# Eight gate blocks of a hybrid encoder step, computed by seven products of quarters

## The chip, the cores and the metric

The kernel runs on one core of one Trainium2 chip. The metric is the device time of one launch, in microseconds (us). The kernel before takes 2427.68 us, the median of three runs (2427.06 to 2428.9). All arithmetic is float32; a float32 product is computed as three TensorE products of split operands (`hi*hi + hi*lo + lo*hi`, each half in the type fp32r).

## What is computed

The reference is one layer of a streaming encoder over T = 1088 tokens (1024 of a prompt, 64 of a running stream), with D = 1024 features:

```python
proj = xn @ w_in      # [z 2048 | xBC 3072 | dt 32 | q 1024 | k 1024 | v 1024 | g_ssm 1024 | g_att 1024]
mix = sigmoid(g_ssm) * (SSD(conv(xBC), dt, z) @ w_branch_ssm) \
    + sigmoid(g_att) * (DiffAttn(q, k, v) @ w_branch_attn)
x = x + mix @ w_out
x = x + ConvFFN(rmsnorm(x))
```

The change concerns the 2048 columns of `proj` called g_ssm and g_att. Cut into blocks of 128 columns they are sixteen **gate blocks**, numbers 0 to 7 for g_ssm and 8 to 15 for g_att. Those from 8 on get `tanh(0.5 g)` when they are made, the others when they are used. All go to a DRAM buffer, `g_sc`, which the last part of the branches reads back.

## The kernel before, in words

Features lie on the 128 partitions, tokens along the free axis. The stages, in order:

- **Values** (v and dt), then the **stage of pairs**. A pair is two blocks of 128 output columns. Its product, [2 row blocks] x [2 halves of the 1024 inputs] x [2 halves of the tokens], is done by Strassen's scheme: seven products of quarters (`in_pair`, L628, products at L650) in place of eight. A quarter product is 4 k-tiles x 3 split terms, for 2 column pieces of 272: 24 TensorE products, so a pair has 168. The seven right operands are made once and stay in SBUF. The left ones are made for each pair from four quarters of weights: GpSimd adds and subtracts them (L564 to L570), ScalarE rounds seven (L420), VectorE takes seven differences (L421), while the pair before multiplies. `INPUT` lists the pairs: four of q, four of k, eight of z. Beside them q and k are normed and rotated (`finishing`). In the last pair the operand b12, which only plain products use, is loaded and split.
- **Attention**: 8 heads x 9 query blocks, 72 units. One unit is scores on TensorE (L1109, L1110), maxima on VectorE, exponentials on ScalarE, a combination on VectorE, transposes (L1138) and the product with the values (L1158).
- **The scan** (SSD): 4 groups x 9 chunks of 128 tokens, 36 steps; three steps make a **span**. `front` makes transposes (L1283), `xx` (L1292), and the masked decays `bc` (GpSimd L1293, ScalarE L1295, VectorE L1296). `back` multiplies (`yi` L1304, `ye` L1310, `stp` L1316) and adds on VectorE (L1311, L1312, L1323). After a span come `gated`, `normed`, `scaled` (L1330 to L1357, GpSimd's L1331 among them).
- **Plain work as filler.** Attention and the scan leave TensorE free, and a generator `filler` gives it plain products (`project` and `branch`: a block of 128 columns is 4 chunks of 272 tokens, 24 products each, L171 to L173). `fill(rate)` is called once in 71 units of attention (`ATT_STEPS`) and 48 times in the scan (`SCAN_STEPS`); a rate of 1 is 363 columns, or 1.33 chunks. `ORDER` says which blocks come: the gate blocks ("g") and the 24 blocks of xBC with their convolution ("c": per chunk a ScalarE copy and two activations, three multiply-adds L999 and one L1001 on VectorE). After them come the 8 blocks of `w_branch_attn` and 8 of `w_branch_ssm`, joined to the filler when the scan reaches span `BRANCH_AT`; the first of these use VectorE to empty PSUM (L235). What is left over runs after the scan (`run(filler)`).
- The third branch product, `w_out`, then the feed-forward pairs (L1615) and `w_down` (L1789).

The framework puts each engine's instructions in one fixed order, by a time line of its own. Each engine then works its list in that order, so on the chip a waiting instruction holds up all that stands behind it. Filler is pulled forward wherever, in that time line, the scan's or attention's own product is not ready.

Of the kernel before, what the change touches and what calls it, by code (L numbers as in the profile page):

```python
# [11 lines left out]
AF = mybir.ActivationFunctionType  # L12
# [5 lines left out]
P = 128  # L18
D = 1024
KT = D // P  # L20
# [26 lines left out]
B_Q, B_K, B_V, B_Z, B_X, B_G = 0, 8, 16, 20, 36, 60  # L47
# [19 lines left out]
ZR = 3  # L67
LAST = 200
FIRST = 4
ATT_STEPS = 1.28  # L70
SCAN_STEPS = 1.4
BRANCH_AT = 4


def group(g):
    return 16 + g, 20 + g, *range(4 * g, 4 * g + 4)


ORDER = (("g", (15, 14)), ("c", group(0)), ("g", (13, 12)), ("c", group(1)), ("g", (11, 10)), ("c", group(2)),
         ("g", (9, 8)), ("c", group(3)), ("g", range(7, 1, -1)))  # L80
INPUT = [(k, i) for k in "qk" for i in range(4)] + [("z", i) for i in range(8)]
Q_DONE = 3

O_MIX, O_FFN, O_CW, O_CB, O_SN, O_D = 0, 8, 16, 112, 136, 152
# [6 lines left out]
def hybrid_layer(ctx: ExitStack, tc: tile.TileContext, xT, xt, prm, cst, rope, wvd, win, wbs, wba, wout, wup, wdn,  # L91
# [3 lines left out]
    act = S.activation  # L95
    load = nc.sync.dma_start
    send = nc.scalar.dma_start
# [4 lines left out]
    def scratch(name, shape, dt=F32):  # L102
        return dram.tile(shape, dt, name=name, tag=name)

    q_st, k_st = (scratch(n, [2 * D, T]) for n in ("q_st", "k_st"))
    q_r, k_r = (scratch(n, [D, T]) for n in ("q_r", "k_r"))
# [5 lines left out]
    z_sc, g_sc = scratch("z_sc", [2 * D, T]), scratch("g_sc", [2 * D, T])  # L112
# [18 lines left out]
    def acc(w):  # L131
        nonlocal at_bank
        pool, n = more
        at_bank = (at_bank + 1) % (n + 2)
        pool, tag = (pool, "mx") if at_bank < n else (pm, "mm")
        t = pool.tile([P, 512], F32, name=tag, tag=tag)
        return t[:, :w]
# [24 lines left out]
    def after(*names):  # L162
        pins = ExitStack()
        for n in names:
            pins.enter_context(tc.issue_after(seen[n].ins))
        return pins
# [256 lines left out]
    def cols(s):  # L423
        return slice(O2[s], O2[s] + W2[s])
# [52 lines left out]
    def row(tag, name, dt=F32):  # L477
        if tag in ("fa", "fs", "fu"):
            w = {"fa": KT * P, "fs": 4 * P, "fu": HT}[tag]
            return rows_l.tile([P, w], dt, name=name, tag=tag, bufs=IN_ROWS[tag])  # L480
        w = {"ss": T}.get(tag, HT)
        return rows_r.tile([P, w], dt, name=name, tag=tag, bufs=IN_ROWS[tag])
# [121 lines left out]
        for y, what in todo:  # L604
            make_left(y, what, blocks)

    FIRST_BLOCK = dict(q=B_Q, k=B_K, z=B_Z)
    LATER = {1: "t1", 3: "t4", 4: "b22"}
    squares, begun_squares = {}, set()

    def blocks_of(n):
        kind, j = INPUT[n]
        return [win[FIRST_BLOCK[kind] + 2 * j + r] for r in range(2)]

# [22 lines left out]
    def in_pair(n):  # L637

        kind, j = INPUT[n]
        u1, u2 = row("fx" if n == 1 else "fu", "u1"), row("fu", "u2")  # L640
        banks, out = {}, {}

        def pile(key, p, s, start):
            if start:
                banks[key, s] = acc(W2[s])
            ps, w, b = banks[key, s], left[n][p], parts[PARTS[p], s]
            for k in range(4):
                c = slice(P * k, P * (k + 1))
                for i, (x, y) in enumerate(((0, 0), (0, 1), (1, 0))):
                    seen["mm"] = PE.matmul(ps, w[x][:, c], b[y][:, k], start=start and k == i == 0, stop=k == 3 and i == 2,  # L650
                                           skip_group_check=not start)
            return ps

        def to(r, c, s):

            if (r, c) not in out:
                out[r, c] = row("fp", "pre")
            a, w = O2[s], W2[s]
            return out[r, c][:, a : a + w]

        def done(r, c):
            cs = slice(HT * c, HT * (c + 1))
            t = out[r, c][:, :HT]
            f = 2 * j + r
            if kind == "z":
                with after("root"):
                    seen["silu"] = act(t, t, AF.Silu)
            else:
                if kind not in squares:
                    squares[kind] = row("ss", "ss")  # L670
                ss = squares[kind][:, cs]
                if (kind, c) not in begun_squares:
                    begun_squares.add((kind, c))
                    act(ss, t, AF.Square)
                else:
                    sq = row("fc", "sq")[:, :HT]
                    act(sq, t, AF.Square)
                    V.tensor_tensor(out=ss, in0=ss, in1=sq, op=ALU.add)
            send(out={"z": z_sc, "q": q_r, "k": k_r}[kind][P * f : P * (f + 1), cs], in_=t)

        at = yield
        for _ in range(14):
            p, s = at
            us = cols(s)
            if p == 0:
                seen["copy"] = S.copy(u1[:, us], pile("a", p, s, True))
            elif p == 1:
                seen["read"] = V.tensor_tensor(out=u2[:, us], in0=pile("b", p, s, True), in1=u1[:, us], op=ALU.add)
            elif p == 3:
                seen["read"] = V.tensor_tensor(out=u1[:, us], in0=pile("b", p, s, False), in1=u1[:, us], op=ALU.add)  # L690
            else:
                r, c, key, start, u = {2: (0, 0, "a", False, None), 4: (1, 1, "c", True, u1), 5: (1, 0, "d", True, u1),
                                       6: (0, 1, "c", False, u2)}[p]
                ps = pile(key, p, s, start)
                if u is None:
                    seen["copy"] = S.copy(to(r, c, s), ps)
                else:
                    seen["read"] = V.tensor_tensor(out=to(r, c, s), in0=ps, in1=u[:, us], op=ALU.add)
                if s == 1:
                    ripe.append(lambda r=r, c=c: done(r, c))  # L700
            at = yield
# [189 lines left out]
    def begun_in(n):  # L891
        u = in_pair(n)
        next(u)
        return u
# [34 lines left out]
    beside = chain(cached_keys(), one_by_one(steps()))  # L929
    for n in range(1, len(INPUT)):  # L930
        blocks = blocks_of(n + 1) if n + 1 < len(INPUT) else None
        u = pairs[1] if n == 1 else begun_in(n)
        for at, (p, s) in enumerate(rest if n == 1 else [(p, s) for p in range(7) for s in range(2)]):
# [7 lines left out]
            take_turn(at)  # L941
            if n + 1 == len(INPUT) and at == 3:
                load_part("b12")
            elif n + 1 == len(INPUT) and at == 9:
                split_part("b12", seen["copy"], seen["read"])
# [62 lines left out]
    def stream():  # L1008
        for kind, which in ORDER:
            if kind == "g" and which[0] < KT:  # L1010
# [20 lines left out]
    with (tc.tile_pool(name="ak", bufs=1) as ak, tc.tile_pool(name="at", bufs=1) as at,  # L1031
# [193 lines left out]
        for h in range(8):  # L1225
# [10 lines left out]
            for x, i in enumerate(ATT_ORDER if h else ATT_FIRST):  # L1236
# [6 lines left out]
                waiting.append((unit, done))  # L1243
                settle(DEEP, ATT_STEPS)
                if h == 0 and x < 3:
# [5 lines left out]
    with (tc.tile_pool(name="sin", bufs=1) as sin, tc.tile_pool(name="sp", bufs=1) as sp,  # L1251
# [177 lines left out]
        for i in scan():  # L1429
            if i == BRANCH_AT and late is not None:  # L1430
                filler, late = late, None
            fill(SCAN_STEPS)
        load(out=conv, in_=conv_o)
# [412 lines left out]
    for i in range(4 * len(DOWN)):  # L1846
        g, last = i // 4, i % 4 == 3 and i + 1 < 4 * len(DOWN)
# [125 lines left out]
```

## Time and profile before

| | us |
|---|---|
| median of three runs | 2427.68 |
| the profiled execution, its own time | 2427.86 |
| its span, first to last instruction | 2426.1 |
| stage of pairs | 117.9 to 473.2 |
| attention | 473.2 to 1076 |
| scan, to the end of its last product and its norm | 1076 to about 1490 |
| third branch product to w_out | to 1705 |
| feed-forward pairs and w_down | to 2426.1 |

The times of the stages are those of the first and last product of the lines named above. An engine's "busy" adds up its instructions; TensorE's products overlap, so what a product costs is read from the spacing of their starts (a stretch divided by the products in it). "PEclk" is the TensorE clock that was granted, 1 being full speed.

### The profile page before, as it was taken

Reading aid. Unit: us, or ns where it says so; the run is one execution under the profiler, and the core shown is the slowest. Engines: PE = TensorE matmul, PEld = TensorE weight load, DVE = VectorE, ACT = ScalarE, POOL = GpSimd, SP = SyncE. Lnnn points to the kernel's source line nnn. Section 1 sums busy time; section 2 is a strip of 40 time slices with the busy share of each in tenths; the row PEclk is TensorE's granted clock in tenths of the full one; section 3 lists DMA queues with packets and bytes.
Section 4 is the critical chain, followed back from the end, with each engine's and each line's share of the span. In section 5 each row is a group of like instructions: output and inputs, shape, how many; then the busy total and the mean of one; then the engine's idle time right before and its main releaser. Section 6 shows DMA issues by size and latency. Waiting matters only on the chain.

```text
span 2426.1 us, 49374 instructions
## 1 busy us (share of the span) xinstructions
PE 2388.9 (98%) x18744; PEld 2316.9 (96%) x18744; DVE 1725.6 (71%) x3090; ACT 1214.9 (50%) x2683; POOL 694.2 (29%) x757
## 2 busy tenths in 40 slices
PE   8999999999999999999999999999999999999998
PEld 8999999999999999998899999999999999999998
DVE  4678987678687786867678665746876766777765
ACT  6444454456566565657665553334533433353442
POOL 0032443111011010115334331013254455543344
PEclk9999999999999999999999999999999999999999
DMA  7774768674545444346897955764124425367976
GB/s 239 275 241 133 266 219 309 198 202 141 158 142 161 135 137 140 113 139 212 275 315 252 347 168 166 214 202 152 62 81 157 146 95 163 127 192 200 252 182 105
DMA packets 296238, 449.78 MB, mean 185 GB/s; under 512 B 36729, under 2 KB 192514, under 8 KB 296002
## 3 DMA queue, kind: packets, MB, share of 16 engines
q1 hardware_dynamic: 268962, 391.46, 50.5%
q0 software_dynamic: 11040, 26.34, 5.4%
q10 hardware_dynamic: 16000, 28.84, 3.2%
q8 instruction: 147, 2.41, 0.4%
q14 instruction: 89, 0.73, 0.1%
HBM read 294.03 MB, written 152.50 MB: 184 GB/s over the span
## 4 chain that ended last, share of the span: by engine, by line
PE 48%; DVE 3%; DMA 1%; issue 1%; ACT 1%; POOL 0%; SPq 0%; POOLq 0%; DVEq 0%; ACTq 0%
PE mx L1615 13%; PE mx L1789 6%; PE mm L1615 5%; PE mx L171 3%; PE mx L173 3%; PE mx L172 3%; PE mm L171 3%; PE mm L173 3%; PE mm L172 3%; PE mm L1789 2%; PE yi L1304 1%; PE ye L1310 1%; PE stp L1316 1%; DMA bc<-a_sc 1%; DVE m L421 1%
## 5 line engine op out<-in xcount | busy, mean ns | idle before, releaser
L171 PE MATMUL mm<-b,w_hi 128*128 128x272 f32 x1576 | 466.2, 296 | 0.0
L173 PE MATMUL mm<-b,w_lo 128*128 128x272 f32 x1576 | 459.8, 292 | 0.0
L172 PE MATMUL mm<-b,w_hi 128*128 128x272 f32 x1576 | 458.3, 291 | 0.0
L171 PEld LDWEIGHTS mm<-b,w_hi 128*128 128x128 f32 x1576 | 297.3, 189 | 6.2 <-issue 5.1
L172 PEld LDWEIGHTS mm<-b,w_hi 128*128 128x128 f32 x1576 | 297.5, 189 | 2.9 <-issue 2.1
L173 PEld LDWEIGHTS mm<-b,w_lo 128*128 128x128 f32 x1576 | 296.9, 189 | 0.7 <-issue 0.2
L999 DVE SCALAR_TENSOR_TENSOR cc<-pre,par,cc 128x272 f32<-128x272 f32 (+1 forms) x288 | 140.1, 490 | 15.4 <-ACT cc L997 12.5
L1615 PE MATMUL mx<-n,wh 128*128 128x272 f32 x1080 | 143.8, 288 | 1.9 <-ACT wh L420 1.0
L1615 PE MATMUL mx<-m,w_hi 128*128 128x272 f32 x752 | 144.6, 289 | 0.2 <-DVE m L421 0.2
L987 POOL COPY pre<-pre 128x3 f32<-128x3 f32 x72 | 23.2, 322 | 418.0 <-DVE cc L1001 195.5
L1615 PEld LDWEIGHTS mx<-n,wh 128*128 128x128 f32 x1080 | 138.3, 188 | 2.5 <-ACT wh L420 1.2
L171 PE MATMUL mx<-b,w_hi 128*128 128x272 f32 x472 | 138.7, 294 | 0.9 <-ACT grs L1341 0.5
L421 DVE TENSOR_TENSOR wh<-w_f,wh 128x512 fp32r<-128x512 f32 (+1 forms) x144 | 138.3, 961 | 0.7 <-ACT wh L420 0.7
L157 DVE TENSOR_TENSOR w_lo<-w_f,w_hi 128x1024 fp32r<-128x1024 f32 (+1 forms) x82 | 102.2, 1247 | 51.1 <-ACT w_hi L156 50.3
L173 PE MATMUL mx<-b,w_lo 128*128 128x272 f32 x472 | 137.7, 293 | 0.8 <-DVE w_lo L157 0.8
L1123 ACT ACTIVATE p_t<-sc,mx 128x512 f32<-128x512 f32 (+6 forms) x144 | 106.2, 740 | 64.2 <-DVE mx L1114 30.1
L172 PE MATMUL mx<-b,w_hi 128*128 128x272 f32 x472 | 135.9, 288 | 0.0
L156 ACT CAST w_hi<-w_f 128x1024 fp32r<-128x1024 f32 (+1 forms) x82 | 85.9, 1048 | 73.2 <-PE mm L172 47.3
L1615 PEld LDWEIGHTS mx<-m,w_hi 128*128 128x128 f32 x752 | 118.1, 188 | 0.4 <-DVE m L421 0.4
L564 POOL TENSOR_TENSOR ws<-w_f 128x512 f32<-128x512 f32 (+1 forms) x47 | 62.3, 1326 | 172.6 <-DMA w_f<-in_wdn_dram 73.1
L1624 ACT ACTIVATE cc<-pre,par 128x544 f32<-128x544 f32 (+1 forms) x44 | 37.2, 845 | 145.4 <-DVE pre L1659 144.5
L1615 PE MATMUL mx<-m,w_lo 128*128 128x272 f32 x376 | 108.3, 289 | 0.0
(462 smaller groups left out, 7085.1 us busy)
## 6 DMA issues: line engine op xcount, KB each, us to landing
w_f<-in_win_dram SPq DMA_DIRECT2D x48, 512.0 KB, 4.2
w_f<-in_wup_dram SPq DMA_DIRECT2D x80, 256.0 KB, 2.9
bc<-a_sc SPq DMA_DIRECT2D x32, 512.0 KB, 5.7
w_f<-in_win_dram SPq DMA_DIRECT2D x60, 256.0 KB, 3.7
b<-y_sc SPq DMA_DIRECT2D x24, 544.0 KB, 8.4
h_sc<-hb SPq DMA_DIRECT2D x44, 272.0 KB, 2.1
ht<-h_sc SPq DMA_DIRECT2D x22, 544.0 KB, 5.2
t_sc<-ht SPq DMA_DIRECT2D x22, 544.0 KB, 2.9
```

The source lines that it names most:

```text
L156: S.copy(hi, w)
L157: V.tensor_tensor(out=lo, in0=w, in1=hi, op=ALU.subtract)
L171: PE.matmul(ps, a_hi, b_hi, start=i == 0, stop=False)
L172: PE.matmul(ps, a_hi, b_lo, start=False, stop=False)
L173: PE.matmul(ps, a_lo, b_hi, start=False, stop=i == n - 1)
L421: V.tensor_tensor(out=lo, in0=src, in1=hi, op=ALU.subtract)
L564: G.tensor_tensor(out=s1, in0=q21, in1=q22, op=ALU.add)
L999: V.scalar_tensor_tensor(cc[:, :m], pre[:, i : i + m], cw(i), cc[:, :m], ALU.mult, ALU.add)
L1123: act(p_t[:n, :nk], sc[c][:n, :nk], AF.Exp, bias=mx[:n, c : c + 1], accum_out=dst)
L1615: PE.matmul(ps, w[x][:, c], b[y][:, k], start=start and k == i == 0, stop=k == 3 and i == 2, skip_group_check=not start)
L1624: act(cc[:, :n], pre[h][:, :n], AF.Identity, bias=col(O_FB + f), scale=cw(0))
L1789: PE.matmul(ps, w[y][:, c], b[z][:, k], start=start and k == j == 0, stop=k == n - 1 and j == 2, skip_group_check=not start)
```

## The change

Gate blocks 4 to 7 and 12 to 15 become four pairs at the end of `INPUT`; the other eight stay plain. The rates of filling fall, and the branch products may start at span 2.

```diff
-ATT_STEPS = 1.28
-SCAN_STEPS = 1.4
-BRANCH_AT = 4
+ATT_STEPS = 1.12
+SCAN_STEPS = 1.17
+BRANCH_AT = 2
...
-ORDER = (("g", (15, 14)), ("c", group(0)), ("g", (13, 12)), ("c", group(1)), ("g", (11, 10)), ("c", group(2)),
-         ("g", (9, 8)), ("c", group(3)), ("g", range(7, 1, -1)))
-INPUT = [(k, i) for k in "qk" for i in range(4)] + [("z", i) for i in range(8)]
+ORDER = (("c", group(0)), ("g", (11, 10)), ("c", group(1)), ("g", (9, 8)), ("c", group(2)), ("c", group(3)), ("g", (3, 2)))
+INPUT = [(k, i) for k in "qk" for i in range(4)] + [("z", i) for i in range(8)] + [("g", i) for i in (2, 3, 6, 7)]
...
-    FIRST_BLOCK = dict(q=B_Q, k=B_K, z=B_Z)
+    FIRST_BLOCK = dict(q=B_Q, k=B_K, z=B_Z, g=B_G)
...
+            elif kind == "g":
+                if f >= KT:
+                    act(t, t, AF.Tanh, scale=0.5)
...
-            send(out={"z": z_sc, "q": q_r, "k": k_r}[kind][P * f : P * (f + 1), cs], in_=t)
+            send(out={"z": z_sc, "q": q_r, "k": k_r, "g": g_sc}[kind][P * f : P * (f + 1), cs], in_=t)
```

Blocks 1 and 0 run after `ORDER`, as before. In the changed kernel lines up to 666 stand one earlier and those from 670 on two later.

**VectorE at the end of the stage of pairs.** `u` and `pre` are a pair's sums, `wh` and `w_lo` lower halves of left operands, `b` is the operand b12. Before, the last z pair:

```order
L690 TENSOR_TENSOR u_5741<-mx,u_5741 128x272 x2
L698 TENSOR_TENSOR pre<-mm,u_5741 128x272 x2
L421 TENSOR_TENSOR b_5813<-b_5813,b_5812 128x1088
L421 TENSOR_TENSOR b_5816<-b_5816,b_5815 128x1088
L698 TENSOR_TENSOR pre<-mx,u_5741 128x272 x2
L157 TENSOR_TENSOR w_lo<-w_f,w_hi 128x1024
```

Now, at the same pair:

```order
L692 TENSOR_TENSOR u_5741<-mx,u_5741 128x272 x2
L700 TENSOR_TENSOR pre<-mm,u_5741 128x272
L420 TENSOR_TENSOR wh<-w_f,wh 128x512
L700 TENSOR_TENSOR pre<-mm,u_5741 128x272
L700 TENSOR_TENSOR pre<-mx,u_5741 128x272 x2
L420 TENSOR_TENSOR wh<-ws_5872,wh 128x512
L700 TENSOR_TENSOR pre<-mm,u_5742 128x272
L420 TENSOR_TENSOR wh<-w_f,wh 128x512
```

The split of b12 has moved to the fourth pair after this one, and the left operands of a further pair stand in its place.

**VectorE in the scan**, between the decays `bc` of step 8 and those of step 9. `state`, `xx` and `y` are the scan's own; `gn`, `grs` its norm; `b_g` empties a chunk of a branch product; `w_lo` splits a block of weights. Before, all ten rows:

```order
L1311 TENSOR_TENSOR y<-ye,e_14788 128x4x128
L1312 TENSOR_TENSOR y<-y,yi 128x4x128
L1311 TENSOR_TENSOR y<-ye,e_14980 128x4x128
L1312 TENSOR_TENSOR y<-y,yi 128x4x128
L1323 TENSOR_TENSOR state<-state,stp 128x512
L1292 TENSOR_TENSOR xx<-tr,dtt 128x1024
L258 SCALAR_TENSOR_TENSOR gn_15201<-grs,gn_15201 128x384
L259 SCALAR_TENSOR_TENSOR grs<-gn_15201,gn_15202 128x384
L1348 SCALAR_TENSOR_TENSOR y<-y,par,grs 128x384 x4
L1296 TENSOR_TENSOR bc<-bc,b_cb 128x1024
```

Now 22 rows stand there. The first ten are two spans' `scaled` (L1350 x8, L1359 x4), one norm and four `b_g`; the last twelve are:

```order
L1325 TENSOR_TENSOR state<-state,stp 128x512
L234 SCALAR_TENSOR_TENSOR b_g<-b_g,mm 128x272
L1313 TENSOR_TENSOR y<-ye,e_15224 128x4x128
L234 SCALAR_TENSOR_TENSOR b_g<-b_g,mx 128x272
L1314 TENSOR_TENSOR y<-y,yi 128x4x128
L156 TENSOR_TENSOR w_lo<-w_f,w_hi 128x1024
L234 SCALAR_TENSOR_TENSOR b_g<-b_g,mm 128x272
L1313 TENSOR_TENSOR y<-ye,e_15388 128x4x128
L156 TENSOR_TENSOR w_lo<-w_f,w_hi 128x1024
L1314 TENSOR_TENSOR y<-y,yi 128x4x128
L1294 TENSOR_TENSOR xx<-tr,dtt 128x1024
L1298 TENSOR_TENSOR bc<-bc,b_cb 128x1024
```

Branch chunks are emptied here that stood two spans later before, and two spans' norms have moved together.

## The prediction

> **What bounds the kernel now.** I read the page's busy times first, then the windows by stage, then who waited for whom, and last the groups of VectorE's lines. The page and four stages (length; busy time and instructions of PE, PEld, DVE, ACT, POOL; clock; DMA share and GB/s):
>
> ```profile
> PE 2388.9 (98%) x18744; PEld 2316.9 (96%) x18744; DVE 1725.6 (71%) x3090; ACT 1214.9 (50%) x2683; POOL 694.2 (29%) x757
> 387.04:473.20 86.16, 85.38 (x675) 84.80 (x674) 65.15 (x109) 37.51 (x69) 25.43 (x23) 1.00 0.72 245
> 473.20:1076.00 602.80, 602.40 (x4643) 579.38 (x4643) 453.29 (x1078) 367.52 (x988) 58.79 (x168) 1.00 0.48 145
> 1076.00:1484.00 408.00, 401.66 (x3247) 365.73 (x3247) 281.12 (x351) 231.01 (x550) 153.25 (x102) 1.00 0.76 251
> 1484.00:1705.00 221.00, 219.31 (x1721) 217.82 (x1721) 136.17 (x240) 92.15 (x161) 29.83 (x27) 1.00 0.63 191
> ```
>
> TensorE is the bound in all of them; VectorE is at 75% in attention and 69% in the scan. What TensorE waited for in attention (first row) and in the scan (total, times, longest):
>
> ```profile
> PE sc L1109 <- DMA q<-q_st: 0.4, 1, 0.4
> ...
> PE tr L1283 <- DMA in<-x_sc: 3.9, 2, 3.1
> PE yi L1304 <- DVE y L1312: 1.4, 1, 1.4
> PE cb L1285 <- ACT grs L1341: 1.0, 1, 1.0
> ```
>
> So a product less is time less, as long as the other engines keep up with the shorter stages.
>
> **What the change removes and adds on TensorE.** Eight gate blocks are 8 x 4 x 24 = 768 plain products less, four pairs 4 x 168 = 672 quarter products more; the fixed order of the changed kernel shows these counts, so the change does what it says. Two z pairs and a long stretch of plain products, all TensorE:
>
> ```profile
> 365.89:408.20 42.31, 42.31 (x339) 42.31 (x338) 33.56 (x56) 20.51 (x39) 16.73 (x17) 1.00 0.93 331
> 452.01:473.20 21.19, 21.19 (x171) 21.19 (x170) 10.73 (x17) 8.70 (x14) 1.17 (x1) 1.00 0.48 152
> 1491.73:1660.10 168.37, 167.20 (x1320) 166.68 (x1321) 95.58 (x178) 66.97 (x121) 13.52 (x12) 1.00 0.71 214
> ```
>
> The first stretch starts 336 products (the few over are from the edges): 42.31/336 = 0.1259 us each. The third starts 1320 in 168.3: 0.1275. Added 672 x 0.1259 = 84.6, removed 768 x 0.1275 = 97.9: **-13.3 us**. Dearer and cheaper stretches of plain products (0.1267 to 0.129) would make it 12.7 to 14.4.
>
> A pair's other work (seven roundings, seven differences, four GpSimd operations, its sums) lies beside the pair ahead of it, as it does for z now: 33.56 of 42.31 on VectorE with the norm of k still beside it, 20.51 on ScalarE. No work on q or k is left beside the new pairs, so I cost it at nothing. Were that cover gone, TensorE would wait for a left operand; the row of the last pair (21.19 long, 21.19 busy) shows none. The move of b12 to the last new pair goes the same way.
>
> **Attention.** 71 calls x (1.28 - 1.12) x 1.3346 x 24 = 364 products leave, 46.4 us: 602.8 becomes 556.4. VectorE keeps its 453 but for four weight splits of 1.3, so 448 of 556, 81%. Its densest stretch now, and the densest of the stage of pairs:
>
> ```profile
> 560.00:600.00 40.00, 40.00 (x307) 38.34 (x307) 35.23 (x90) 29.26 (x75) 3.74 (x14) 1.00 0.42 134
> 280.00:320.00 40.00, 39.88 (x316) 39.63 (x315) 38.30 (x61) 19.46 (x36) 19.39 (x17) 1.00 0.78 252
> ```
>
> 40 us become 36.9, and 35.2 of them is 95%; the second row shows VectorE at 96% beside a TensorE that hardly waits. Four stretches are this dense (every second head). If VectorE can't pass 88%, each costs 3.1: 0 to 12 us. TensorE waits for nothing here today, so I take the low end: **+1**.
>
> **The scan.** Six spans, step 6 to step 24 (from one `yi` to the next but two):
>
> ```profile
> 1146.30:1182.20 35.90, 33.49 (x272) 29.93 (x271) 25.91 (x33) 23.81 (x60) 12.35 (x9) 1.00 0.68 225
> 1182.20:1217.20 35.00, 35.00 (x286) 32.38 (x285) 23.73 (x26) 18.83 (x42) 16.24 (x11) 1.00 0.93 319
> 1217.20:1250.30 33.10, 33.10 (x272) 30.30 (x271) 26.26 (x33) 18.06 (x44) 10.31 (x8) 1.00 1.08 363
> 1250.30:1286.50 36.20, 36.20 (x294) 32.91 (x293) 28.86 (x38) 24.50 (x54) 15.30 (x11) 1.00 0.77 252
> 1286.50:1318.50 32.00, 32.00 (x262) 29.39 (x261) 27.21 (x36) 16.02 (x34) 9.88 (x7) 1.00 0.79 254
> 1318.50:1354.60 36.10, 36.10 (x294) 33.30 (x293) 26.21 (x36) 15.80 (x40) 15.38 (x10) 1.00 0.81 262
> ```
>
> 208.3 us for 18 steps, with 1080 plain products by the order: 137.7, so a step's own products take (208.3 - 137.7)/18 = 3.92. In the changed order filler runs ahead: 151 plain products stand before `yi` of step 7, and only 646 between it and `yi` of step 24. For those 17 steps TensorE needs 646 x 0.1275 + 17 x 3.92 = 149.1 us. VectorE's rows of the scan (count, busy and mean ns of one; idle):
>
> ```profile
> L1296 DVE TENSOR_TENSOR bc<-bc,b_cb 128x1024 f32<-128x1024 f32 (+1 forms) x36 | 58.1, 1615 | 11.3 <-ACT b_cb L1288 6.6 <-ACT bc L1295 4.6
> L1292 DVE TENSOR_TENSOR xx<-tr,dtt 128x1024 f32<-128x1024 f32 (+1 forms) x36 | 43.8, 1218 | 15.2 <-PE tr L1283 11.4 <-issue 3.8
> L1330 DVE SCALAR_TENSOR_TENSOR y<-in,par,y 128x384 f32<-128x384 f32 (+1 forms) x48 | 31.4, 709 | 0.2
> L157 DVE TENSOR_TENSOR w_lo<-w_f,w_hi 128x1024 fp32r<-128x1024 f32 x22 | 29.0, 1316 | 25.0 <-ACT w_hi L156 25.0
> L1348 DVE SCALAR_TENSOR_TENSOR y<-y,par,grs 128x384 f32<-128x384 f32 (+1 forms) x44 | 26.0, 646 | 0.2
> L1323 DVE TENSOR_TENSOR state<-state,stp 128x512 f32<-128x512 f32 x32 | 21.8, 682 | 1.6 <-PE stp L1316 1.4
> L1311 DVE TENSOR_TENSOR y<-ye,e 128x512 f32<-128x512 f32 (+1 forms) x32 | 20.9, 654 | 29.1 <-PE ye L1310 26.3 <-DMA in<-x_sc 1.7 <-DMA y_sc<-y 1.2
> L1312 DVE TENSOR_TENSOR y<-y,yi 128x512 f32<-128x512 f32 (+1 forms) x32 | 20.8, 650 | 2.1 <-PE yi L1304 1.6
> L1357 DVE TENSOR_TENSOR y<-y,zin 128x768 fp32r<-128x768 f32 (+1 forms) x12 | 14.3, 1190 | 0.0
> L235 DVE SCALAR_TENSOR_TENSOR b_g<-b_g,mm 128x272 f32<-128x272 f32 x22 | 9.4, 432 | 16.0 <-PE mm L173 13.4 <-DMA b_g<-g_sc 2.6
> L259 DVE SCALAR_TENSOR_TENSOR grs<-gn,gn 128x384 f32<-128x384 f32 (+1 forms) x11 | 9.1, 824 | 0.2
> ```
>
> and, from the same groups kept apart by shape:
>
> ```profile
> L258 DVE SCALAR_TENSOR_TENSOR gn<-grs,gn 128x384 f32<-128x384 f32 x8 | 4.4, 556 | 14.6 <-ACT gn L257 14.6
> ```
>
> For these 17 steps the new order holds, by the old line numbers, 17 each of L1296 and L1292, 20 L1330, 8 L157, 24 L1348, 15 L1323, 16 L1311, 15 L1312, 12 L1357, 31 L235, 6 L259, 7 L258: 155.4 us. So VectorE has more to do than TensorE. Some 14 us of it need no `yi` from step 7 on (the first rows of the long block shown with the change: 8 L1348, 4 L1357, a norm, 5 L235, a state), and can be done beside the 151 products. At the 96% above the rest keeps up: 155.4/0.96 - 14 = 148. At 88%, which the window 1280 to 1320 of the scan reaches without a wait of TensorE's, it is 162.6: 13.5 us too long.
>
> ```profile
> 1280.00:1320.00 40.00, 40.00 (x333) 37.03 (x332) 35.21 (x40) 19.41 (x40) 16.18 (x10) 1.00 0.82 265
> ```
>
> Behind a waiting `yi` stand all the filler and the transposes of the next step, so each such wait is lost. Between 0 and 13.5 I take the middle, **+6**. What the earlier branch products ask for is in this count (L235) but for their loads, which are a rival below.
>
> How long L1296 takes beside GpSimd (duration min/median/max):
>
> ```profile
> L1296 DVE TENSOR_TENSOR bc<-bc,b_cb x36: 673/1226/3618, 1094.5 to 1461.2; 128x1024 f32<-128x1024 f32 x32, 64x512 f32<-64x512 f32 x4
> ```
>
> Its mean is 1615, a median 1226: 14 us of stretch over the scan. The Trainium skill (GPSIMD Engine Reference, Specifications) says why: GpSimd shares its SBUF interfaces with VectorE, to the cost of instructions with two SBUF inputs, as L1296 is. By that rule the stretch grows with GpSimd's share as the stage shrinks, 14 x 408/363, which adds 1.7 us of VectorE work; by fixed durations it adds nothing. The trace agrees that L1296 stretches.
>
> **After the scan** 7 chunks of filler are left instead of 9, 2 x 24 x 0.1275 = 6.1 us less cover for the last norm. The last norm's rows (first and last start):
>
> ```profile
> L219 SPq DMA_DIRECT2D b<-y_sc x8: 359/385/604, 1493.4 to 1508.8; - x8
> L1351 SPq DMA_DIRECT2D y_sc<-y x3: 359/360/371, 1448.4 to 1496.5; - x3
> ```
>
> The last store is issued 12 us before the last load of it, so 6 us less still fits: nothing.
>
> **Sum.** Against the profiled execution's own 2427.86 (0.2 above the median): 2427.9 - 13.3 + 1 + 6 = 2421.6, say **2421 us**.
>
> **Rivals.** *All stays hidden*: VectorE passes 96%, no wait is added: 2414.6. For it: TensorE's 0.4 us of waits in attention.
>
> *Slower, by the scan's disorder*: where the order before is irregular too (spans 1 and 2), TensorE stands still and its clock falls. The window (clock in the third figure from the end):
>
> ```profile
> 1113.80:1146.30 32.50, 29.35 (x230) 26.34 (x229) 23.76 (x29) 23.80 (x61) 19.00 (x12) 0.95 0.48 146
> ```
>
> and in the order of time (start, length, instruction, idle before it):
>
> ```profile
> 1125.39 1.09 PE L1283 MATMUL tr<-con,in 128*128 128x128 f32 x4 [3.15 <-DMA in<-x_sc]
> 1126.51 0.43 PE L171 MATMUL mm<-b,w_hi 128*128 128x272 f32 x1
> 1126.73 0.43 PE L172 MATMUL mm<-b,w_hi 128*128 128x272 f32 x1
> ```
>
> 3.15 + 2.41 us idle, and products 0.22 apart for eight of them, 0.8 more: 6.4 us for two spans. The new order is irregular through span 8. Eight spans at 3.2 are 25.6, 19.2 more than now: 2434.8 with attention's 1. It decides the sign at 13.3 + 6.4 over eight spans, 2.5 us a span. Against it: 4 of the 6.4 come from one load at the scan's start. The Trainium skill (TensorE: Matmul & The Clock Gate, Why this matters for your kernels) asks for no idle gap above about 3 us, else the clock halves. The trace agrees at 3.15; waits in smaller pieces would cost by that rule only themselves.
>
> *Loads*: the branch operands (363 GB/s in the row 1217 to 1250) come two spans earlier, beside the scan's own. Were the 3.9 of waits for `in` paid once more, with the slow clock: 2427.
>
> **Chances.** Forecast 0.45; all hidden 0.22; slower 0.23; loads 0.10. 0.2% is 4.9 us, about what a measurement of this kernel can tell. Faster by more: all of the hidden case and four fifths of the forecast, 0.58. Within: the rest of the forecast, the loads and a little of the slower case, 0.22. Slower: 0.20. The range: down to the hidden case with 14.4 and the start's 3.15 of waits gone, 2411; up to the slower case with 2 us of attention more, 2437.
>
> **What would show it.** Stage of pairs 84.6 longer with PE busy throughout; attention 46 shorter; waits of `yi` and `cb` in steps 8 to 24; after step 24 spans of 30 us with none. Wrong, if the waits fall in attention, at the new pairs, or sum to more than 13 us.

## The result, and the profile after

The changed kernel takes 2423.43 us (median of 16 runs, 2418.43 to 2426.93); the kernel before, beside it, 2428.1 (16 runs, 2424.96 to 2431.32). The ratio is 0.9975, 95% interval 0.9969 to 0.9982: 4.4 to 7.5 us faster. The forecast was 2421, or 6.3 us faster. By the medians 8.6 of the products' 13.3 us are given back, where the forecast had 7, and not all for the forecast's reasons.

The page's first part for the changed kernel. Its profiled execution took 2425.83 us, with a span of 2424.0:

```profile
PE 2379.3 (98%) x18648; PEld 2306.1 (95%) x18648; DVE 1750.6 (72%) x3150; ACT 1217.8 (50%) x2695; POOL 731.4 (30%) x773
```

96 products less in all, and TensorE still at 98%. A kernel's runs scatter by several us, so single profiles are compared stage by stage, each stage cut at its own marks: the stage of pairs from its first to its last product, attention from the first scores to the last transposes, the scan from the first `yi` to the last, and what follows up to the first sum of the feed-forward's norm (L1523, now L1525). First the three stages of before, then those of after (length; busy time and instructions of PE, PEld, DVE, ACT, POOL; clock; DMA share; GB/s). TensorE's idle time is the length less the first busy time.

```profile
117.90:473.00 355.10, 349.97 (x2723) 344.08 (x2722) 285.33 (x461) 173.85 (x322) 122.94 (x108) 1.00 0.69 229
...
479.77:1082.50 602.73, 601.94 (x4638) 578.74 (x4638) 452.47 (x1072) 367.90 (x989) 58.69 (x167) 1.00 0.48 145
1096.70:1476.07 379.37, 373.81 (x3039) 339.85 (x3039) 269.90 (x336) 218.41 (x523) 147.12 (x99) 1.00 0.76 250
```

```profile
117.70:559.50 441.80, 434.68 (x3395) 428.67 (x3395) 321.38 (x530) 200.49 (x374) 140.85 (x124) 1.00 0.61 203
...
566.03:1132.42 566.39, 563.85 (x4322) 540.47 (x4322) 444.00 (x1069) 358.04 (x973) 69.50 (x168) 1.00 0.48 148
1145.49:1478.87 333.38, 325.12 (x2647) 289.75 (x2646) 265.72 (x329) 206.90 (x502) 152.00 (x99) 1.00 0.82 273
```

| stage | length before | after | plain products less | worth at 0.1275 | lost | TensorE idle before | after |
|---|---|---|---|---|---|---|---|
| pairs | 355.1 | 441.8 | none (672 quarter products more) | | | 5.1 | 7.1 |
| attention | 602.7 | 566.4 | 316 | 40.3 | 4.0 | 0.8 | 2.5 |
| scan | 379.4 | 333.4 | 395 | 50.4 | 4.4 | 5.6 | 8.3 |
| after the scan | 184.1 | 178.4 | 48 | 6.1 | 0.4 | | |

The loss sits in two places, attention and the scan. In this profile the stage of pairs also grew by 86.7 us, 2.1 more than its products' 84.6. Over the profiles of all kernels with these four pairs it took 438.4 to 443.8 us, so I count that as scatter. Idle time explains 1.8 of attention's 4.0 and 2.7 of the scan's 4.4; the rest is that TensorE's busy time fell by only 0.1205 and 0.1233 us per plain product there.

Six spans of the scan after, from step 12 on, and what TensorE waited for in it (total, times, longest):

```profile
1253.50:1283.30 29.80, 28.15 (x222) 24.49 (x221) 29.61 (x37) 17.11 (x42) 12.20 (x9) 1.00 0.72 224
1283.30:1309.50 26.20, 24.56 (x203) 21.58 (x202) 21.06 (x29) 19.01 (x45) 17.15 (x10) 1.00 0.90 295
1309.50:1336.60 27.10, 25.64 (x211) 22.76 (x210) 26.20 (x35) 13.39 (x31) 7.13 (x6) 1.00 0.87 280
1336.60:1367.60 31.00, 29.57 (x240) 26.69 (x239) 24.01 (x32) 18.59 (x44) 17.62 (x10) 1.00 1.08 367
1367.60:1404.30 36.70, 35.25 (x280) 31.17 (x279) 25.27 (x32) 22.08 (x57) 11.80 (x10) 1.00 0.81 279
1404.30:1431.50 27.20, 27.20 (x228) 25.08 (x227) 19.14 (x18) 18.43 (x47) 16.53 (x10) 1.00 0.65 213
```

```profile
PE yi L1306 <- DVE y L1314: 3.1, 2, 1.6
PE tr L1285 <- DVE xx L1294: 2.3, 3, 1.4
PE stp L1318 <- DVE state L1325: 1.0, 2, 0.8
PE yi L1306 <- ACT y L1316: 0.7, 1, 0.7
PE cb L1287 <- ACT b_cb L1290: 0.6, 1, 0.6
```

Of the 8.3 us of waits 6.2 stand where they were forecast, between steps 12 and 24, mostly on VectorE; 1.5 stand in the span behind step 24, where none was forecast. VectorE is at 97 to 99% of the first and third of these spans. That looked like a VectorE whose work bounds the scan. It doesn't, as the experiments show. The wait for `in` at the scan's start, 3.9 us in the profile of before, isn't there.

### The profile page after: what moved, and what is told of

The parts are those of the page before. It is cut to its first block, busy times and chain, and to the rows that moved or that the text cites. A ratio compares the mean times of both kernels' runs of the same rounds, so it can differ in the third digit from the quotient of the medians.

```text
span 2424.0 us, 49267 instructions
## 1 busy us (share of the span) xinstructions
PE 2379.3 (98%) x18648; PEld 2306.1 (95%) x18648; DVE 1750.6 (72%) x3150; ACT 1217.8 (50%) x2695; POOL 731.4 (30%) x773
## 4 chain that ended last, share of the span: by engine, by line
PE 44%; DVE 6%; DMA 3%; issue 2%; ACT 1%; POOL 1%; SPq 0%; POOLq 0%; DVEq 0%; ACTq 0%
PE mx L1617 13%; PE mx L1791 6%; PE mm L1617 5%; PE mm L170 2%; PE mm L172 2%; PE mm L171 2%; PE mx L170 2%; PE mm L1791 2%; PE mx L172 2%; PE mx L171 2%; PE yi L1306 1%; PE stp L1318 1%; PE ye L1312 1%; DMA b<-y_sc 1%; DMA m_sc<-b_g 1%
## 5 line engine op out<-in xcount | busy, mean ns | idle before, releaser
L170 PE MATMUL mm<-b,w_hi 128*128 128x272 f32 x1376 | 408.7, 297 | 0.0
L172 PE MATMUL mm<-b,w_lo 128*128 128x272 f32 x1376 | 404.2, 294 | 0.0
L171 PE MATMUL mm<-b,w_hi 128*128 128x272 f32 x1376 | 403.0, 293 | 0.0
L170 PEld LDWEIGHTS mm<-b,w_hi 128*128 128x128 f32 x1376 | 259.5, 189 | 5.7 <-issue 3.4
L171 PEld LDWEIGHTS mm<-b,w_hi 128*128 128x128 f32 x1376 | 259.6, 189 | 4.5 <-issue 3.1
L172 PEld LDWEIGHTS mm<-b,w_lo 128*128 128x128 f32 x1376 | 259.1, 188 | 3.6 <-issue 2.5
L1617 PE MATMUL mx<-m,w_hi 128*128 128x272 f32 x792 | 152.3, 290 | 1.2 <-ACT m L419 1.2
L420 DVE TENSOR_TENSOR wh<-w_f,wh 128x512 fp32r<-128x512 f32 (+1 forms) x156 | 151.6, 973 | 0.7 <-ACT wh L419 0.7
L170 PE MATMUL mx<-b,w_hi 128*128 128x272 f32 x416 | 122.9, 296 | 2.0 <-ACT w_hi L155 1.5
L172 PE MATMUL mx<-b,w_lo 128*128 128x272 f32 x416 | 121.5, 294 | 0.0
L171 PE MATMUL mx<-b,w_hi 128*128 128x272 f32 x416 | 121.4, 292 | 0.0
L156 DVE TENSOR_TENSOR w_lo<-w_f,w_hi 128x1024 fp32r<-128x1024 f32 (+1 forms) x74 | 92.8, 1256 | 22.5 <-ACT w_hi L155 22.1
L419 ACT CAST wh<-w_f 128x512 fp32r<-128x512 f32 (+1 forms) x156 | 95.2, 613 | 27.0 <-POOL w_f L569 8.3
```

The source lines that it names most:

```text
L156: V.tensor_tensor(out=lo, in0=w, in1=hi, op=ALU.subtract)
L170: PE.matmul(ps, a_hi, b_hi, start=i == 0, stop=False)
L171: PE.matmul(ps, a_hi, b_lo, start=False, stop=False)
L172: PE.matmul(ps, a_lo, b_hi, start=False, stop=i == n - 1)
L419: S.copy(hi, src)
L420: V.tensor_tensor(out=lo, in0=src, in1=hi, op=ALU.subtract)
```

## The experiments

**The theory** at the start was: the gain is products times spacing, and what is given back is VectorE running full in the scan, with a little in attention. **The rivals**: the loss is attention's, or the pairs', or thin filling costs nothing by itself.

**1. More filler in the scan, less in attention.**

```diff
-ATT_STEPS = 1.12
-SCAN_STEPS = 1.17
+ATT_STEPS = 1.05
+SCAN_STEPS = 1.275
```

Expected:

> Attention 1.05 and the scan 1.275 a call, so some 150 plain products move from attention to the scan. If the loss of the change sits in the scan, where VectorE is at 97 to 99% of spans 4 to 7 (the theory), the scan's 8 us of waits fall to 2 to 4, attention gains 1 to 2 of its own, and the time is 2419 to 2421 against 2423.4 for the changed kernel. If it sits in attention (the rival, by the 4 us that its length lost against its products), the scan's relief counts less than attention's new waits: 2425 to 2428. If thin filling costs nothing in either and only the pairs were dearer, 2423 to 2424.

Measured: 2429.6 us, ratio 1.0009 (0.9999 to 1.0018): the whole gain is gone. Attention and the scan, in its profile:

```profile
560.90:1113.80 552.90, 546.80 (x4186) 523.34 (x4186) 440.16 (x1062) 356.18 (x965) 59.07 (x166) 1.00 0.49 147
1127.20:1480.50 353.30, 344.95 (x2782) 308.41 (x2782) 271.35 (x331) 212.18 (x512) 158.73 (x99) 1.00 0.79 263
```

136 products more in the scan, and TensorE's idle time there is 8.4 us, not the 2 to 4 that a full VectorE would have left; attention's rises to 6.1. The theory missed, and the rival of attention came nearer, though 2429.6 lies beyond its 2425 to 2428 too. The scan is 353.3 us long, 19.9 more than in the changed kernel, for products worth 17.3. (The profiled run was this kernel's quickest, so its stages show less than the median's loss.)

**2. The rates alone, on the kernel before.**

```diff
-ATT_STEPS = 1.28
-SCAN_STEPS = 1.4
+ATT_STEPS = 1.12
+SCAN_STEPS = 1.17
```

Expected:

> The kernel before with the two smaller rates alone: all sixteen gate blocks stay plain, no new pairs, the same number of products, the unused filler runs after the scan. If thinner filling is what gives part of the saving back (the theory), this is slower than the kernel before by what the changed kernel lost in attention and the scan, 6 to 9 us: 2434 to 2437. If the loss came from the pairs or from the branch's earlier products (the rivals), it is within 1.5 us of 2428.1.

Measured: 2452.71 us beside 2427.57, ratio 1.0100 (1.0086 to 1.0114): 25 us slower, beyond anything expected. The scan, with two stretches of its first 70 us, and two groups of VectorE's rows from 1055 to 1160:

```profile
1055.00:1090.00 35.00, 30.27 (x248) 25.08 (x248) 32.30 (x37) 28.91 (x77) 21.02 (x18) 1.00 0.52 179
1090.00:1125.00 35.00, 21.95 (x130) 15.75 (x130) 30.76 (x40) 22.16 (x47) 15.72 (x15) 0.79 0.48 152
...
1055.08:1411.58 356.50, 335.64 (x2688) 297.98 (x2688) 288.80 (x363) 226.54 (x543) 162.57 (x117) 0.97 0.71 233
```

```profile
L999 DVE SCALAR_TENSOR_TENSOR cc<-pre,par,cc 128x272 f32<-128x272 f32 (+1 forms) x30 | 23.5, 809 | 1.8 <-POOL conv_o L994 1.2 <-ACT cc L997 0.6
...
L1001 DVE SCALAR_TENSOR_TENSOR cc<-pre,cc 128x272 f32<-128x272 f32 (+1 forms) x11 | 6.7, 613 | 3.7 <-ACT pre L1000 3.7
```

With the old order of blocks and slower filling the convolutions aren't done when the scan begins: 30 us of their VectorE work stand beside the scan's first spans. TensorE is idle for 20.9 us of the scan and runs part of it at half clock (0.79 in the second stretch). In the changed kernel no convolution stands in the scan. So I read the order of blocks that came with the change, convolutions first, as what makes the low rates possible; no run has that order and these rates without the pairs. As a test of thin filling alone this run says nothing: the edit brought a cost of its own.

**3. Less VectorE work in the scan: the gates' multiplication left out.** ScalarE copies the products out of PSUM instead, so the result lacks the gates.

```diff
-                        if not beside:
+                        if not beside or not adds:
                             S.copy(to, ps)
```

Expected:

> Leaves out the multiplication of the first branch's products by their gates: ScalarE copies them out of PSUM instead of VectorE (0.43 us each, 31 of them beside steps 7 to 24 of the scan, 13 us less of VectorE's 155). If VectorE's work is the bound of these steps (the theory), the scan's waits fall by 4 to 6 us: 2417.5 to 2419.5. If the waits come from the order of the work, or from loads, and not from VectorE's sum (the rival), they stay: 2422.5 to 2424.

Measured: 2419.94 us, ratio 0.9967 (0.9955 to 0.9980). The scan in its profile:

```profile
1143.50:1473.88 330.38, 324.45 (x2647) 290.13 (x2646) 255.78 (x297) 215.34 (x532) 151.23 (x98) 0.99 0.83 275
```

Idle 5.9 us against 8.3, and 3.0 us shorter. It leans towards the theory, but its interval overlaps that of the changed kernel, and two further runs went against it:

**4. The differences of the scaled outputs to GpSimd.**

```diff
-                V.tensor_tensor(out=lo[:, js], in0=y[:, js], in1=hi[:, js], op=ALU.subtract)
+                G.tensor_tensor(out=lo[:, js], in0=y[:, js], in1=hi[:, js], op=ALU.subtract)
```

Expected:

> The differences of the scaled outputs (y less its rounding, 128x768, 1.19 us each, 12 in the scan) go from VectorE to GpSimd, so VectorE has 14 us less in the scan and GpSimd some 20 to 30 more. If VectorE's work is the bound there and GpSimd's spare time can be used (the theory), the waits fall by 3 to 6 us: 2417.5 to 2420.5. If the two engines share what they read through (the rival, as the stretched rows of bc beside GpSimd suggest), VectorE's other rows grow by as much and the time is 2422.5 to 2426.

Measured: 2424.07 us, ratio 0.9980 (0.9971 to 0.9990): nothing won. In the scan VectorE's busy time fell by 11.0 us and GpSimd's rose by 25.5.

**5. The term of D left out.**

```diff
-            for j in range(4):
-                V.scalar_tensor_tensor(y[:, j], xs[:, j, :w], col(O_D + 4 * g + j), y[:, j], ALU.mult, ALU.add)
```

Expected:

> Leaves out the term of D in the scan's output (the four products with x per span, 0.7 us each): some 14 us less of VectorE beside steps 7 to 24 and nothing added on another engine, where moving the differences to GpSimd took VectorE work away and won nothing. If VectorE's work bounds these steps (the theory), the scan's waits fall by 4 to 6 us: 2417.5 to 2419.5. If it is the order and GpSimd's share of the chain (the rival), 2422 to 2424.

Measured: 2426.16 us, ratio 0.9988 (0.9977 to 0.9999), no better than with the term. The scan of experiment 4, then that of 5 and what TensorE waited for in it:

```profile
1145.72:1479.35 333.63, 325.96 (x2647) 290.81 (x2646) 254.67 (x317) 206.89 (x504) 177.47 (x111) 0.99 0.82 274
```

```profile
1142.08:1475.71 333.63, 324.93 (x2646) 290.66 (x2646) 238.72 (x285) 206.82 (x502) 146.09 (x98) 0.99 0.82 272
```

```profile
PE mm L172 <- DVE w_lo L156: 2.8, 1, 2.8
PE yi L1306 <- ACT y L1316: 2.6, 1, 2.6
PE stp L1318 <- DVE state L1325: 1.3, 1, 1.3
```

27 us of 266 are gone from VectorE, with nothing put on another engine, and the scan is as long as before the edit (333.6 against 333.4), idle 8.7 us, in a profiled run (2420.95) that was one of this kernel's two quickest. One stretch of 3.4 us ran at half clock here and none in the changed kernel; that can hide 1.7 us, not the 4 to 6 that the theory asked for. The waits only stand elsewhere: at a split of weights, at a copy of ScalarE's. VectorE's sum is not the bound of the scan at this filling. The theory falls here. The framework set a new order for this kernel: 683 plain products stand between `yi` of step 7 and that of step 24, where the changed kernel has 646, and TensorE waits 4.5 us there against 6.2, but 4.2 ahead of step 7 against 0.6. So it is not shown that the order of VectorE's work has no part in the waits. Why experiment 3, with 10 us less on VectorE, had a scan 3 us shorter stays open too.

**6. Less filler in the scan, more in attention**, the opposite of the first experiment.

```diff
-ATT_STEPS = 1.12
-SCAN_STEPS = 1.17
+ATT_STEPS = 1.19
+SCAN_STEPS = 1.065
```

Expected:

> The opposite of the first experiment: attention 1.19, the scan 1.065 a call, some 150 products or 20 us of cover moved from the scan to attention. If VectorE's work bounds the scan (the theory), its length can't follow: 10 to 18 us of new waits there against 2 won in attention, 2431 to 2439. If the waits are single places of bad order that come and go with the position of the products (the rival), 2421 to 2426, as the first experiment's 2429.6 with more filler in the scan suggests.

Measured: 2436.82 us, ratio 1.0031 (1.0020 to 1.0042). The scan:

```profile
1169.61:1495.64 326.03, 310.09 (x2504) 274.31 (x2503) 276.20 (x328) 204.09 (x498) 154.00 (x99) 0.99 0.80 264
```

143 products less than the changed kernel has there, worth 18.2 us, shorten the scan by 7.4. TensorE is idle for 15.9 us. The number is the theory's, though its reason has fallen: the scan does stop following its products.

**7. Half and one and a half doses.** Four blocks by pairs:

```diff
-ATT_STEPS = 1.12
-SCAN_STEPS = 1.17
-BRANCH_AT = 2
+ATT_STEPS = 1.2
+SCAN_STEPS = 1.285
+BRANCH_AT = 3
...
-ORDER = (("c", group(0)), ("g", (11, 10)), ("c", group(1)), ("g", (9, 8)), ("c", group(2)), ("c", group(3)), ("g", (3, 2)))
-INPUT = [(k, i) for k in "qk" for i in range(4)] + [("z", i) for i in range(8)] + [("g", i) for i in (2, 3, 6, 7)]
+ORDER = (("c", group(0)), ("g", (11, 10)), ("c", group(1)), ("g", (9, 8)), ("c", group(2)), ("c", group(3)), ("g", range(7, 1, -1)))
+INPUT = [(k, i) for k in "qk" for i in range(4)] + [("z", i) for i in range(8)] + [("g", i) for i in (6, 7)]
```

Expected:

> Half the dose: four gate blocks by pairs, rates 1.2 and 1.285, the branch from span 3. The products alone give 384 x 0.1275 less 336 x 0.1259, 6.65 us. If the give-back comes from VectorE being full in the scan (the theory), it is small at half the dose (0 to 2 us, since VectorE is then under 95% of the scan's spans), and the time lies 5 to 6.5 us under the kernel before: 2421.5 to 2423, no worse than the whole change. If the give-back goes with the blocks moved (the rival: the pairs, or each thinner call, cost a fixed share), it is half of 7: about 3 us under the kernel before, 2425.

Twelve blocks (with the activation table's preload kept ahead of the last two):

```diff
-ATT_STEPS = 1.12
-SCAN_STEPS = 1.17
-BRANCH_AT = 2
+ATT_STEPS = 1.0
+SCAN_STEPS = 1.05
+BRANCH_AT = 1
...
-ORDER = (("c", group(0)), ("g", (11, 10)), ("c", group(1)), ("g", (9, 8)), ("c", group(2)), ("c", group(3)), ("g", (3, 2)))
-INPUT = [(k, i) for k in "qk" for i in range(4)] + [("z", i) for i in range(8)] + [("g", i) for i in (2, 3, 6, 7)]
+ORDER = (("c", group(0)), ("g", (9, 8)), ("c", group(1)), ("c", group(2)), ("c", group(3)))
+INPUT = [(k, i) for k in "qk" for i in range(4)] + [("z", i) for i in range(8)] + [("g", i) for i in (1, 2, 3, 5, 6, 7)]
```

Expected:

> One and a half doses: twelve gate blocks by pairs, rates 1.0 and 1.05, the branch from span 1. The products alone give 19.9 us. If VectorE bounds the scan (the theory), nearly all of what is taken from the scan beyond the changed kernel is lost there: scan waits of 14 to 20 us, attention's 4 to 8, total 2422 to 2430, no gain over the changed kernel. If the give-back is a fixed share of the dose (the rival, 7 of 13.3), the time is 2418.5 to 2420.

Measured: four blocks 2428.62 us beside 2428.96, ratio 1.0003 (0.9995 to 1.0012); twelve blocks 2438.87, ratio 1.0043 (1.0031 to 1.0055). Attention and the scan with four, then the scan with twelve:

```profile
522.70:1108.70 586.00, 582.04 (x4471) 558.50 (x4471) 448.59 (x1071) 363.76 (x981) 59.87 (x168) 1.00 0.48 146
1121.90:1475.90 354.00, 350.94 (x2855) 316.99 (x2857) 266.81 (x334) 213.74 (x515) 154.18 (x99) 1.00 0.79 263
```

```profile
1162.50:1485.60 323.10, 305.46 (x2407) 266.83 (x2406) 267.73 (x331) 199.75 (x488) 153.16 (x98) 0.97 0.79 262
```

Both forecasts for four blocks were too good, and both for twelve: 2438.87 lies 9 us above the upper end of the slower (2422 to 2430). The scan of four blocks is fine (3.1 us idle). Its attention isn't: 168 products less are worth 21.4, the stage is only 16.7 shorter, and it waits 4.0 us, more than in the changed kernel with its lower rate. So attention's loss doesn't follow the rate. Another 3 us of its profile are in the feed-forward stage, which the edit doesn't touch; I leave them as scatter.

The scan's length against its plain products, one kernel for each count (experiment 2 is left out for the convolutions in its scan); the last column counts the stretches of 3.4 us at half clock (see the end):

| kernel | plain products in the scan | length | shorter than the row above, for each product less | TensorE idle | stretches at half clock |
|---|---|---|---|---|---|
| before | 1891 | 379.4 | | 5.6 | 1 |
| four blocks | 1709 | 354.0 | 0.139 | 3.1 | 1 |
| experiment 1 | 1632 | 353.3 | 0.009 | 8.4 | 1 |
| changed | 1496 | 333.4 | 0.146 | 8.3 | 0 |
| experiment 6 | 1353 | 326.0 | 0.051 | 15.9 | 2 |
| twelve blocks | 1248 | 323.1 | 0.028 | 17.6 | 6 |

A product less is worth its full time at first, and a fifth of it at the end. Between them the length doesn't follow the count alone: experiment 1 has 77 products less than four blocks and is 0.7 us shorter. The rows differ in `ORDER` and `BRANCH_AT` too. Experiment 1, the changed kernel and experiment 6 differ in the rates alone, and give 0.146 and then 0.051. So the bend is seen below the changed kernel's 1496 products; what experiment 1 lost at 1632 is not explained by the count. Part of the last row is the clock: six stretches at half clock can be worth 10 us.

**8. The branch at span 4 again**, all else as changed.

```diff
-BRANCH_AT = 2
+BRANCH_AT = 4
```

Expected:

> BRANCH_AT 4 again instead of 2, all else as changed: the branch's products and its loads start two spans later, and what filler is then missing leaves calls without plain products. If the bound is VectorE's sum over the steps (the theory), work is only put off, and spans 2 and 3 run without filler: the waits grow by 5 to 15 us at one place, 2428 to 2438. If the early branch itself does the harm, by its loads or by irregular order (the rival), the waits fall and the time is 2418 to 2421.

Measured: 2424.69 us, ratio 0.9981 (0.9972 to 0.9989), the changed kernel's own. Both expectations rested on a false premise: the plain gate blocks aren't used up by span 4, so the order of products doesn't change; in the trace every engine's instructions stand as in the changed kernel. The run serves as a repeat: two builds of one order came out at 0.9975 and 0.9981. It shows too that the new `BRANCH_AT` is no part of what the change does.

**9. The price of the pairs by themselves.** The changed kernel with rates, `BRANCH_AT` and `ORDER` of before:

```diff
-ATT_STEPS = 1.12
-SCAN_STEPS = 1.17
-BRANCH_AT = 2
+ATT_STEPS = 1.28
+SCAN_STEPS = 1.4
+BRANCH_AT = 4
...
-ORDER = (("c", group(0)), ("g", (11, 10)), ("c", group(1)), ("g", (9, 8)), ("c", group(2)), ("c", group(3)), ("g", (3, 2)))
+ORDER = (("g", (15, 14)), ("c", group(0)), ("g", (13, 12)), ("c", group(1)), ("g", (11, 10)), ("c", group(2)),
+         ("g", (9, 8)), ("c", group(3)), ("g", range(7, 1, -1)))
```

Expected:

> The four new pairs, but the rates, the order and all sixteen plain blocks of the kernel before: eight gate blocks are computed twice, so nothing is saved. The price of the pairs alone. If a pair is its 168 products and its other work hides (the theory), this is 84.6 us over the kernel before, 84 to 86: 2512 to 2514, with attention and the scan at their lengths of before. If the pairs bring something beyond their products (the rival: roundings, differences or stores that aren't hidden, the move of b12), 88 to 92 more: 2516 to 2520.

Measured: 2509.47 us beside 2428.96, ratio 1.0329 (1.0316 to 1.0343), that is 77 to 83 us more, a little under the theory's 84 to 86. The stages of its profiled run:

```profile
116.70:556.00 439.30, 434.33 (x3396) 428.65 (x3395) 321.05 (x530) 200.43 (x374) 142.68 (x124) 1.00 0.61 205
563.20:1164.90 601.70, 601.68 (x4638) 578.74 (x4638) 452.21 (x1071) 368.33 (x989) 58.29 (x167) 1.00 0.48 145
1180.30:1558.60 378.30, 372.86 (x3037) 338.55 (x3039) 271.06 (x336) 219.03 (x525) 147.33 (x99) 1.00 0.76 250
```

The stage of pairs is 84.2 longer, TensorE's busy time in it 84.4 more for 672 products, its idle time 5.0 as before; attention and the scan are 1.0 shorter each. So the pairs cost their products, and the rival falls. That the other three runs were 1 to 7 us quicker than the profiled one isn't explained by any trace. The wait for `in` at the scan's start is missing here too, in a scan that is that of before: its absence is no work of the change.

**10. The same blocks, spread evenly.** One plain gate block ahead of each group of convolutions:

```diff
-ORDER = (("c", group(0)), ("g", (11, 10)), ("c", group(1)), ("g", (9, 8)), ("c", group(2)), ("c", group(3)), ("g", (3, 2)))
+ORDER = (("g", (11,)), ("c", group(0)), ("g", (10,)), ("c", group(1)), ("g", (9,)), ("c", group(2)), ("g", (8,)), ("c", group(3)), ("g", (3, 2)))
```

Expected:

> The changed kernel with one plain gate block (11, 10, 9, 8) ahead of each conv group, where it has two behind the first and two behind the second group; all rates and counts as changed. Its conv groups 2 and 3 stand back to back, and a conv block brings VectorE work that a gate block doesn't. If attention's 4 us of give-back come from VectorE work that stands too close together (the theory), attention's length falls by 2 to 4: 2420 to 2421.5. If they come from attention's own chain beside fewer products, wherever the blocks stand (the rival), the time stays within 1.5 us of the changed kernel's 2423.4.

Measured: 2419.14 us (6 runs, 2416.51 to 2420.42) beside 2429.99, ratio 0.9958 (0.9942 to 0.9974): 6 to 14 us under the kernel before, and 4 under the changed kernel, though the intervals of the two touch. Attention and the scan:

```profile
564.25:1127.55 563.30, 562.48 (x4322) 540.39 (x4322) 442.46 (x1068) 358.39 (x972) 67.47 (x167) 1.00 0.50 149
1140.61:1473.13 332.52, 325.13 (x2646) 289.69 (x2646) 266.24 (x329) 206.25 (x501) 151.60 (x98) 1.00 0.82 273
```

The same 4322 instructions in attention, 3.1 us shorter; idle 0.8, as before the change. Of the 4.0 lost in attention 0.9 is left. The stages bear it out: five profiles of kernels with the changed kernel's order and rates (it and experiments 3, 4, 5 and 8) have 566.1 to 567.4 us of attention, two with the even order (this and the next) 563.3 and 563.6. So that loss came from the order of the blocks. That it was the two groups of convolutions back to back, and no other place of the order, is argued and not shown: in experiment 2, at the same rate, gate blocks stand between all groups, and attention still lost 3.5 us (560.9 for 355 products less). This is the fastest version of the study that computes the whole result.

**11. A second PSUM buffer for `yi`**, on the even order.

```diff
-        more = psi, 1
...
-            yi = psi.tile([P, 4, P], F32, name="yi", tag="yi")
+            yi = psi.tile([P, 4, P], F32, name="yi", tag="yi", bufs=2)
```

Expected:

> The even order, with two PSUM buffers for yi in the scan instead of one; the third bank of the plain products there goes for it. Less VectorE work alone won nothing, and the scan's largest waits (yi for the sum that empties its one buffer) are waits for a place in VectorE's queue. If the single buffer is what waits (the theory), 1.6 to 3 us of waits at yi go: 2416 to 2417.5 against 2419.1 of the even order. If the wait moves to the next single buffer, tr, stp or cb (the rival): 2418.5 to 2420.5. If plain products on two banks wait for their emptying: 2422 or more, with waits at mm.

Measured: 2432.55 us, ratio 1.0023 (1.0014 to 1.0033). What TensorE waited for in the scan:

```profile
PE mm L170 <- DVE b_g L234: 3.0, 1, 3.0
PE gst L1339 <- POOL zin L1335: 3.0, 1, 3.0
PE tr L1284 <- DMA in<-x_sc: 2.5, 2, 2.3
PE mm L172 <- DVE w_lo L156: 1.5, 2, 1.3
PE yi L1305 <- ACT y L1315: 1.1, 1, 1.1
```

The wait of `yi` for VectorE's sum is gone, as the theory had it, and the plain products now wait for VectorE to empty one of their two banks: the last of the three cases came. The time is 13 us worse than the even order's. Here the third bank was worth more than the second `yi`. The waits alone don't make the 13 us. The scan grew by 8.0 with only 2.1 of it idle time:

```profile
1141.45:1481.95 340.50, 331.00 (x2645) 294.99 (x2644) 269.28 (x328) 207.07 (x501) 150.04 (x98) 0.98 0.81 267
```

The clock was halved for four stretches of 3.4 us in it and for two more right behind it, none in the even order's; at up to 1.7 us each that is some 10 of the 13.

## Why the prediction was right

- **Products, -13.3: right.** Its two halves can be checked only for the pairs: 84.6 forecast, 84.7 and 84.4 in TensorE's busy time in two kernels. Their other work is hidden, as costed.
- **Attention, +1: mis-sized, 4.0.** The step asked whether the same VectorE work fits a shorter stage. It left out that the new `ORDER` moves the work: the last two groups of convolutions stand back to back. Spread evenly (experiment 10), attention loses 0.9, which is the +1.
- **The scan, +6: near in size (4.4), wrong in its reason.** The step failed where it says that "VectorE has more to do than TensorE" and makes that the bound. Its 155.4 us are counts times mean durations, but VectorE's instructions overlap as TensorE's products do: in its own row of L1348, 44 instructions of 646 ns are busy for 26.0 us, not 28.4. In the changed kernel the durations between `yi` of step 7 and that of step 24 do add up to 141.8 us, the forecast's 155.4 less the 14 done ahead, yet VectorE is busy for 129.6 (third figure) of 150.5. Even with the 14 done ahead that is less than the 149.1 of TensorE's count:

```profile
1217.10:1367.60 150.50, 144.32 (x1177) 127.98 (x1176) 129.64 (x166) 94.50 (x228) 73.24 (x46) 1.00 0.87 288
```

  Taking 27 us from VectorE changed nothing, accordingly. Nor does the loss stand where it was put: at 0.1275 a product, these steps lost 2.9 us (1032 products in 196.8 us before, 646 in 150.5 now) and not 6, and the steps behind them 2.0 (624 in 121.5, 528 in 111.2), where nothing was forecast; ahead of them 0.5 was won. What the runs show in its place is that, with less filler, the scan's own waits are less covered, and that each wait that is shortened is followed by the next, on VectorE, ScalarE, GpSimd or a load. Which chain does it, and whether the scan has a floor near the shortest one seen (323.1 us), isn't settled.
- **After the scan, 0: right**, 5.7 us shorter for 48 products.
- **The split between stages was off**: 316 products left attention and 395 the scan's stage, where 364 and 354 were counted from the rates; attention became 36.3 us shorter, not 46. The framework places filler by its own time line, so a rate gives the sum and not the place.
- **The rivals.** That all stays hidden fell: both stages lost. The slower case, 2.5 us a span over eight spans, did not come: the waits are 8.3 us in all and the clock stayed up. Its mechanism was real, though: experiment 2 (20.9 us idle, half clock) and twelve blocks (17.6, clock 0.97) are that case. Loads did not show: no wait for `in` in the changed kernel.

So -13.3 + 4.0 + 4.4 = -4.9 us. The medians are 4.7 apart and the ratio says 6.1; the two profiles themselves are only 2.1 apart, mostly because of the 2.1 us in the stage of pairs. The forecast had 1 and 6 in place of 4.0 and 4.4, errors of opposite sign from reasons that didn't hold: that their sum came so near is luck in part.

## What to carry to other kernels

Work that fills another stage's waits loses its worth as it gets scarce: measure the stage at two or three amounts of filler before pricing its removal, and expect a bend. Price an engine's work by the spacing of its instructions or by its busy time, not by durations added up. An engine at 97% of a stretch isn't shown to be the bound until taking work from it shortens the stretch. Where a list of blocks feeds the filler, its order is a cost of its own: here the right order was worth 4 us, and low rates with the old one lost 25 on the kernel before.

## What the runs showed of the hardware

**The clock is granted by fixed windows.** In all fourteen traces the stretches at half clock begin on a grid of 3.413 us and last one or more of its cells. What counts is TensorE's share of one cell, not the length of a gap. Two kernels, cell by cell; first that with four blocks, around one wait of 1.71 us:

```profile
1166.12:1169.54 3.42, 1.71 (x18) 1.13 (x15) 3.42 (x5) 1.79 (x3) 1.18 (x1) 1.00 0.03 10
1169.54:1172.95 3.41, 3.41 (x16) 3.41 (x17) 3.41 (x5) 0.31 (x2) 1.50 (x1) 0.50 0.68 214
```

then that without the term of D, around one wait of 2.84 us:

```profile
1190.16:1193.56 3.40, 2.06 (x15) 1.62 (x13) 3.40 (x3) 1.68 (x7) 2.65 (x3) 1.00 1.07 370
1193.56:1196.97 3.41, 1.89 (x15) 1.89 (x16) 3.41 (x5) 0.34 (x2) 0.00 (x0) 1.00 1.09 381
1196.97:1200.38 3.41, 3.41 (x19) 2.22 (x18) 0.74 (x2) 0.02 (x1) 0.00 (x0) 1.00 1.07 406
```

The shorter wait fell into one cell, half of it, and the next cell ran at 0.50. The longer one lay across two, which were busy for 0.61 and 0.55, and cost no clock. Between 100 and 2400 us of the fourteen traces, of cells at full clock 29 of 30 that were busy below 0.48 were followed by a halved one, 13 of 23 from 0.48 to 0.55, 2 of 23 up to 0.60, and none of 9286 above. The Trainium skill (TensorE: Matmul & The Clock Gate, What's actually happening) has the free-running window of 3413 ns, and the traces agree; it lets the clock fall after an idle window, where here half an idle window is enough. The prediction's use of its 3 us for a gap was too kind: waits of 1.7 us can already cost 1.7 more, by where the grid happens to lie, and that differs from run to run.

**A wait moves.** In the scan the longest wait was at `yi` for VectorE, at `w_lo`, at `gst` for GpSimd, at `ye` or at `mm`, according to the edit, while the stage's length stayed within 1 us over three of them (333.4 in the changed kernel, 333.6 in experiments 4 and 5).
